# Three row blocks on four weight chunks at the start, an earlier weight load before the second attention, and two pinned orders

## The chip, the cores and the metric

The kernel runs on one core of a Trainium2 chip. The metric is the device time of one execution in microseconds (us); lower is better. The core has a matrix engine (TensorE; PE in the profile, its weight loads PEld), three other compute engines (VectorE = DVE, ScalarE = ACT, GpSimd = POOL) and SyncE (SP), whose queue issues most DMA transfers. Each engine runs its own instructions strictly in the order in which the program put them; semaphores tie the engines together.

## The reference

Two encoder layers on x of 1024 rows by 1024 columns, all in float32. Layer 0 mixes tokens by latent attention, layer 1 by differential attention; after each there is a gated feed-forward. What the change touches first is the first product of layer 0 and the normalisation behind it:

```python
h = x @ w_in                                   # 1024 x 704
c_q, c_kv, k_rope = jnp.split(h, [384, 640], axis=-1)
c_q = _rmsnorm(c_q, g_q)
c_kv = _rmsnorm(c_kv, g_kv)
...
h = _layernorm(ALPHA * h + mix, ln_mix_g[i], ln_mix_b[i])
h = _layernorm(ALPHA * h + _swiglu(h, ffn_w_gu[i], ffn_w_down[i]), ln_ffn_g[i], ln_ffn_b[i])
...
h = x @ w_in                                   # layer 1: 1024 x 3072, q, k and v of 8 heads
gate, up = jnp.split(x @ w_gu, 2, axis=-1)     # the feed-forward
return (jax.nn.silu(gate) * up) @ w_down
```

## The kernel before

**Precision.** TensorE multiplies in a rounded 32-bit format. Every operand is split into a rounded high part (a cast, nearly always on ACT) and the rest (a subtraction on DVE or POOL), and each product is made of three: high by high, high by low, low by high. So each operand costs a load, a cast and a subtraction before TensorE has all of it.

**First projection** (`load_x`, `load_w_in`, `project`, `latents`, `turn_c`). The 1024 rows are 8 row blocks of 128, and the 1024 columns of x are 8 chunks k of 128. One chunk of w_in is 128 x 704 (352 KB); one row block of x is 128 x 1024 (512 KB), laid out so that columns 128k to 128k+127 are the operand of chunk k. `project` accumulates a row block's 128 x 704 result in two PSUM banks, hq (384 columns, tag m) and hk (320 columns, tag t), with six matmuls for each chunk: xh by wh, xh by wl, xl by wh, for hq and hk each, so 48 for a row block. There are three banks of each of the tags m and t. Row blocks 0 and 1 are projected together, chunk by chunk; blocks 2 to 7 follow one at a time. The loads are issued by SP in program order: x of block 0 for chunks 0 and 1, w chunk 0 in two pieces, x of block 1 for chunks 0 and 1, w chunk 1, the rest of block 0, w chunk 2, the rest of block 1, w chunks 3 to 7. `latents` squares and sums hq and hk on ACT, scales them on DVE into a tile cn (two buffers) with a power on POOL between, and so frees the banks; `turn_c` transposes cn.

**Order.** The program is a list of operations; a scheduler that simulates the engines puts each engine's share in order at build time. `behind(i, j)` pins one operation behind another without a wait. `tc.high_priority` moves a part forward.

**End of layer 0.** `ffn` ends with eleven products of its last block (`dw` from the operands `op_w` and `op_h`), which POOL prepares from `t4` (L520) while `next_x` loads the first value weights of layer 1 (`wbv`). The rows of layer 0's result are normalised by `layer_norm` (L184 is its last step) and transposed by `to_xT` into the operand of layer 1 (`xTp_f`). The weights of head 0's query (tile `wb`) are loaded by `proj_b`, the first time it is called; the subtraction of that load (L137 on POOL) is pinned behind the power of the first normalised row block.

**Start of a feed-forward.** `load_pre` prepares the gate operands n = 0 to 5, `gates` multiplies them in pairs, `prepare` and `consume` do the rest of each n. One pin in `load_pre` puts the cast of operand 1 of n = 3 behind `ends["p1"]`, which is the last plain copy of a gate product.

Of the kernel before, what the change touches and what calls it, by code (L numbers as in the profile page):

```python
# [16 lines left out]
P = 128  # L17
S = 1024
D = 1024
# [23 lines left out]
def trunk(  # L43
# [54 lines left out]

    banks("ps0", PS_BUFS_A)
    dr = ctx.enter_context(tc.tile_pool(name="dr", bufs=1, space=DRAM))  # L100

# [26 lines left out]
    def load_w(src, cols, name, hi=None, lo=None, eng=None, raw=None, ins=False):  # L128

        if raw is None:  # L130
            raw = wp.tile([P, 1024], F32, tag="wr", bufs=2, name=f"r_{name}")
        nc.sync.dma_start(raw[:, :cols], src)
        if hi is None:
            hi = wp.tile([P, 1024], F32R, tag="wh", name=f"h_{name}")
            lo = wp.tile([P, 1024], F32R, tag="wl", name=f"l_{name}")
        A.copy(hi[:, :cols], raw[:, :cols])
        j = (eng or G).tensor_tensor(lo[:, :cols], raw[:, :cols], f32(hi[:, :cols]), ALU.subtract)  # L137
        return (hi, lo, j.ins) if ins else (hi, lo)
# [397 lines left out]
    def ffn(side, xo, xst, pending, layer, x_src, x_dst, lng, lnb, next_x, spare=()):  # L536
# [53 lines left out]
        def prepare(n, pr):  # L590
# [8 lines left out]
            if pr == ("5" if n < 2 else "6"):  # L599
                i = V.tensor_tensor(a21, a21, a22, ALU.add).ins  # L600
                if n < 2:
                    behind(i, ends["x"])
            if pr == ("3" if n < 2 else "6"):
                V.tensor_tensor(a11, a21, a11, ALU.subtract)
# [13 lines left out]
        def consume(n, pr):  # L618
# [3 lines left out]
            if pr in "12":  # L622
# [10 lines left out]
                else:  # L633
                    A.activation(g0, acc[n, "a"], AF.Silu)
                return
# [17 lines left out]
            if pr == "6":  # L653
                V.tensor_tensor(u2, p1, acc[n, "b"], ALU.add)
                for c in acc[n, "cs"] if n < 2 else ():
# [427 lines left out]
    with tc.tile_pool(name="a0", bufs=2, side="right") as pool:  # L1083
        xs, win = {}, []

        def load_x(tb, k0=0, k1=KD):

            if tb not in xs:
                xs[tb] = [
                    pool.tile([P, D], dt, tag=tag, name=f"{tag}_{tb}", bufs=2 if tag == "x" else 3)  # L1090
                    for dt, tag in ((F32, "x"), (F32R, "xh"), (F32R, "xl"))
                ]
            c = slice(k0 * P, k1 * P)
            xt, xh, xl = (t[:, c] for t in xs[tb])
            nc.sync.dma_start(xt, xt_in[tb, :, c])
            i, j = A.copy(xh, xt).ins, V.tensor_tensor(xl, xt, f32(xh), ALU.subtract).ins
# [4 lines left out]
        def load_w_in(k, n=1):  # L1101
# [4 lines left out]
            if n == 1:  # L1106
                *_, j = load_w(w_in_a[k], 704, f"win{k}", hi, lo, G if k > 2 and k % 2 else V, raw, True)
                return j
# [7 lines left out]
        load_w_in(0, 2)  # L1116
        load_x(1, 0, 2)
        load_w_in(1)
        load_x(0, 2, 8)
        load_w_in(2)  # L1120
        load_x(1, 2, 8)
        third = load_w_in(3)
        for k in range(4, KD):
            load_w_in(k)
        nc.sync.dma_start(ident, c_ident)
        with tc.issue_after(third):
# [5 lines left out]
        def project(tbs):  # L1132
            ms = [(ps_m(f"hq{tb}"), ps_t(f"hk{tb}")) for tb in tbs]
            for k in range(KD):
                kc = slice(k * P, (k + 1) * P)
                wh, wl = win[k]
                for tb, (hq, hk) in zip(tbs, ms):
                    _, xh, xl = xs[tb]
                    for lh, w, st, sp_ in (
                        (xh, wh, k == 0, False), (xh, wl, False, False), (xl, wh, False, k == KD - 1)  # L1140
                    ):
                        T.matmul(hq[:, :384], lh[:, kc], w[:, 0:384], start=st, stop=sp_)  # L1142
                        T.matmul(hk[:, :320], lh[:, kc], w[:, 384:704], start=st, stop=sp_)
            return ms

        def latents(tb, hq, hk):
            junk = pool.tile([P, 384], F32, tag="junk", name=f"junk{tb}")
            ssq = small(f"ssq{tb}", 2)
            A.activation(junk, hq[:, :384], AF.Square, accum_out=ssq[:, 0:1])
            ends["squares", tb] = A.activation(junk[:, :256], hk[:, :256], AF.Square, accum_out=ssq[:, 1:2]).ins  # L1150
            ve = small(f"cve{tb}", 2)
# [3 lines left out]
            G.tensor_tensor(rs, ve, mhalf, ALU.pow)  # L1155
            cn = pool.tile([P, 768], F32, tag="cn", name=f"cn{tb}")
            ra = pool.tile([P, 64], F32, tag="ra", name=f"ra{tb}")
# [22 lines left out]
        done = []  # L1180
        for tbs in ((0, 1), (2,), (3,), (4,), (5,), (6,), (7,)):
            for tb in tbs:
                if tb > 1:
                    load_x(tb)
# [8 lines left out]
    gs, nlam = cst[:, 16:17], cst[:, 24:25]  # L1193
    V.memset(ones, 1.0 / P)

    def constants():
# [14 lines left out]
    with ast as st:  # L1211
# [4 lines left out]
        for t, src in ((cos, c_cos), (sin, c_sin), (ba, c_bias_a)):  # L1216
            nc.sync.dma_start(t, src)
        vt, qr, qn, kn, wts, lt, pts = {}, {}, {}, {}, {}, {}, {}
# [127 lines left out]
    def next_x():  # L1346
        pool = xst.enter_context(tc.tile_pool(name="xp0", bufs=1, side="right", reuse_waits="tile"))
        wts["v", 0] = [load_w(w_b_v[0, kh], 1024, f"wbv0_{kh}") for kh in range(2)]
        return new_xT(pool, "f0")

# [17 lines left out]
    with ExitStack() as st:  # L1368
# [280 lines left out]
```

## Time and profile before

| what | value |
|---|---|
| median of 3 runs | 2256.71 us (2256.47 to 2257.42) |
| the profiled execution: its time | 2256.85 us |
| its span, first to last instruction | 2255.1 us |
| mean granted TensorE clock over the span | 0.999 |
| TensorE busy | 2235.1 us, 99% |
| DVE, ACT, POOL busy | 68%, 45%, 34% |
| share of the 16 DMA engines, mean rate | 35% and 128 GB/s |

The busy share says how much of the span an engine had an instruction under way; only TensorE is near the whole. So time can be won or lost only where TensorE waits or runs at a lower clock, and the rows in the section below show the few places where it does.

### The profile page before, as it was taken

The numbers are of one execution on the slowest core, as the hardware profiler recorded it, in microseconds if no ns is written. First come the engines' busy times: TensorE is split into PE (matmuls) and PEld (weight loads), VectorE is DVE, ScalarE is ACT, GpSimd is POOL, SyncE is SP. The second block draws the span as 40 slices with busy tenths as digits, with TensorE's granted clock in tenths as the row PEclk, the third lists the DMA queues.
The fourth block names the chain that finished last, engine by engine and source line by source line (L and its number), as shares of the span: only waits on it lengthen the run. The fifth ranks groups of instructions, "written<-read, shape, count | busy, mean of one in ns | idle before, by whom it ended". The sixth has DMA issues, their size and how long they took to land.

```text
span 2255.1 us, 31061 instructions
## 1 busy us (share of the span) xinstructions
PE 2235.1 (99%) x11410; PEld 1911.9 (85%) x11410; DVE 1543.9 (68%) x2894; ACT 1014.0 (45%) x2097; POOL 773.5 (34%) x626
## 2 busy tenths in 40 slices
PE   9999999999999999999999999999999999999998
PEld 8899998888888888888989898988888888888886
DVE  5676765696666657767576666577787656658778
ACT  4455664352333334444465656455432333334444
POOL 2232341114434440456432424222014444430551
PEclk9999999999999999999999999999999999999999
DMA  5010125334535338454310212063344232238453
GB/s 204 14 35 32 42 71 187 141 130 146 181 126 201 121 131 327 177 201 150 103 44 32 64 34 68 24 224 131 121 148 163 82 110 101 102 112 331 160 183 149
DMA packets 105545, 287.76 MB, mean 128 GB/s; under 512 B 7968, under 2 KB 30112, under 8 KB 94896
## 3 DMA queue, kind: packets, MB, share of 16 engines
q1 hardware_dynamic: 101552, 277.44, 34.6%
q0 software_dynamic: 3840, 8.33, 1.4%
q8 instruction: 90, 1.47, 0.3%
q14 instruction: 63, 0.52, 0.1%
HBM read 204.47 MB, written 77.07 MB: 125 GB/s over the span
## 4 chain that ended last, share of the span: by engine, by line
PE 96%; DVE 2%; DMA 1%; ACT 1%; issue 1%; POOL 0%; SPq 0%; DVEq 0%; POOLq 0%; ACTq 0%
PE gb L563 16%; PE gc L563 11%; PE ga L563 10%; PE dw L889 8%; PE dx L889 5%; PE zp_a L431 4%; PE s_a L220 3%; PE s_b L220 3%; PE dv L889 3%; PE dy L889 3%; PE bp L145 3%; PE bp L143 3%; PE bp L144 3%; PE o_a L263 2%; PE o_b L263 2%; PE hq L1142 2%
## 5 line engine op out<-in xcount | busy, mean ns | idle before, releaser
L519 ACT CAST op_g<-gr 128x512 fp32r<-128x512 f32 x240 | 146.8, 621 | 377.9 <-PE gb L563 185.8
L520 POOL TENSOR_TENSOR op_g<-gr,op_g 128x512 fp32r<-128x512 f32 x104 | 144.9, 1398 | 253.8 <-ACT op_g L519 141.6
L520 DVE TENSOR_TENSOR op_h<-rh,op_h 128x512 fp32r<-128x512 f32 x152 | 140.1, 948 | 51.1 <-ACT op_h L519 51.1
L563 PE MATMUL ga<-xh_m,op_g 128*128 128x512 f32 x512 | 168.2, 389 | 0.0
L889 PE MATMUL dw<-op_w_t,op_h 128*128 128x512 f32 x660 | 151.2, 390 | 0.0
L519 ACT CAST op_h<-rh 128x512 fp32r<-128x512 f32 x152 | 91.9, 619 | 124.3 <-PE dx L889 32.6
L889 PEld LDWEIGHTS dw<-op_w_t,op_h 128*128 128x128 f32 x660 | 123.6, 188 | 25.8 <-DVE op_h L520 0.3
L228 ACT ACTIVATE l_b<-l_b,mx_b 128x256 f32<-128x256 f32 (+7 forms) x128 | 99.4, 777 | 74.8 <-DVE mx_b L223 72.9
L520 DVE TENSOR_TENSOR op_g<-gr,op_g 128x512 fp32r<-128x512 f32 x136 | 112.9, 833 | 17.1 <-ACT op_g L519 16.8
L520 POOL TENSOR_TENSOR op_w_b<-rw_b,op_w_b 128x512 fp32r<-128x512 f32 x44 | 64.7, 1493 | 172.1 <-ACT op_w_b L519 172.0
L1451 POOL TENSOR_SCALAR l_b<-l_b,rb,cst 128x128 f32<-128x128 f32 (+3 forms) x64 | 52.5, 821 | 200.5 <-DVE rb L1450 188.0
L889 PE MATMUL dx<-op_w_b,op_h 128*128 128x512 f32 x528 | 120.3, 389 | 0.0
L889 PEld LDWEIGHTS dx<-op_w_b,op_h 128*128 128x128 f32 x528 | 99.1, 188 | 20.6
L563 PE MATMUL gb<-t2h_f,op_g 128*128 128x512 f32 x352 | 115.4, 390 | 0.4 <-DVE op_g L520 0.4
L563 PE MATMUL gc<-t1h_f,op_g 128*128 128x512 f32 x352 | 115.6, 389 | 0.0
L563 PE MATMUL gb<-t4h_f,op_g 128*128 128x512 f32 x352 | 115.5, 389 | 0.0
L563 PE MATMUL gc<-b22h_f,op_g 128*128 128x512 f32 x352 | 115.4, 389 | 0.0
L563 PE MATMUL gb<-t3h_f,op_g 128*128 128x512 f32 x352 | 115.2, 389 | 0.0
L563 PEld LDWEIGHTS ga<-xh_m,op_g 128*128 128x128 f32 x512 | 96.1, 188 | 19.9
L520 POOL TENSOR_TENSOR op_g<-s,op_g 128x512 fp32r<-128x512 f32 x40 | 55.2, 1381 | 166.5 <-ACT op_g L519 158.6
L143 PE MATMUL bp<-xT_f,h_wb 128*128 128x512 f32 x256 | 101.8, 398 | 0.0
L144 PE MATMUL bp<-xT_f,h_wb 128*128 128x512 f32 x256 | 101.6, 397 | 0.0
(389 smaller groups left out, 6689.5 us busy)
## 6 DMA issues: line engine op xcount, KB each, us to landing
gr<-in_w_gu SPq DMA_DIRECT2D x44, 1024.0 KB, 6.8
rh<-h_dr SPq DMA_DIRECT2D x28, 1024.0 KB, 4.8
h_dr<-sh SPq DMA_DIRECT2D x22, 1024.0 KB, 5.0
h_dr<-hp SPq DMA_DIRECT2D x22, 768.0 KB, 4.1
tt<-in_w_dn SPq DMA_DIRECT2D x22, 512.0 KB, 8.8
rh<-h_dr SPq DMA_DIRECT2D x12, 768.0 KB, 4.4
wo_dr<-op_pwo SPq DMA_DIRECT2D x16, 512.0 KB, 3.3
z<-xs_dr SPq DMA_DIRECT2D x16, 512.0 KB, 11.1
```

What stands on the lines that cost most here:

```text
L143: T.matmul(ps_out, lh, rh, start=(i == 0), stop=False)
L144: T.matmul(ps_out, lh, rl, start=False, stop=False)
L145: T.matmul(ps_out, ll, rh, start=False, stop=(i == n - 1))
L220: T.matmul(s[:, :w], lh, rh[:, ks], start=(j == 0), stop=(j == len(q_pass) - 1))
L228: ends["exp"] = A.activation(l[:, :n], l[:, :n], AF.Exp, bias=mx, scale=-1.0, accum_out=sm).ins
L263: T.matmul(po[:, c], a, b[:, j % 2, c], start=st, stop=sp_, skip_group_check=True)
L431: T.matmul(m, a[:, h, :], self.wo[h][w][:, c], start=(start and h == heads[0] and a is oh and w == 0), stop=(stop and h == heads[-1] and a ...
L519: turns["cast"] = A.copy(hi, src).ins
L520: return eng.tensor_tensor(lo, src, f32(hi), ALU.subtract).ins
L563: T.matmul(o, w[:, a, k * P:(k + 1) * P], x[b][:, k, :], start=(first and k == 0 and (a, b) == (0, 0)), stop=(k == 3 and a == 1), skip_gro ...
L889: T.matmul(o, h[:, a, c], w[:, b_], start=(first and (a, b_) == (0, 0)), stop=(last and a == 1), skip_group_check=True,).ins for a, b_ in ...
L1451: G.tensor_scalar(l1[:, :n], l1[:, :n], r[:, 1:2], nlam, ALU.mult, ALU.mult)
```

## The change

It has five parts. (1) Eight matmuls of the constant tile `ones` with itself (`spin`, 128 x 128, float32) stand at the head of TensorE's order; their result is used by nothing, and the memset of `ones` moves to the start. (2) Row blocks 0, 1 and 2 are projected together for chunks 0 to 3, and then one after the other for chunks 4 to 7; loads, casts and subtractions of x follow in smaller pieces, the low part of weight chunk 7 moves from POOL to DVE, and later loads (x of blocks 3 to 7, cos, sin, the bias) stand behind the last weight load. (3) The squares in `latents` go to the tile cn, not to a scratch tile; raw x has three buffers. (4) Head 0's query weights are loaded in `next_x`, with the value weights; the pin on their subtraction is gone. (5) In the feed-forward, the cast pinned behind `ends["p1"]` now stands behind the Silu of n = 0, and the addition that opens n = 3 stands behind the first reading of n = 1's product.

```diff
@@ trunk: start
     banks("ps0", PS_BUFS_A)
+    V.memset(ones, 1.0 / P)
+    spin = ps.tile([P, 512], F32, tag="s", bufs=ps_bufs[0], name="spin")
+    for _ in range(8):
+        T.matmul(spin[:, :P], ones, ones, start=True, stop=True)
@@ load_w
-        nc.sync.dma_start(raw[:, :cols], src)
+        ends["load"] = nc.sync.dma_start(raw[:, :cols], src).ins
+        if "w" in ends:
+            behind(ends["load"], ends["w"])
@@ ffn: prepare, pr == "6"
                 if n < 2:
                     behind(i, ends["x"])
+                elif n == 3:
+                    behind(i, ends["read"])
@@ ffn: consume, pr in "12" and pr == "6"
-                    A.activation(g0, acc[n, "a"], AF.Silu)
+                    i = A.activation(g0, acc[n, "a"], AF.Silu).ins
+                    if n == 0:
+                        ends["p1"] = i
...
-                V.tensor_tensor(u2, p1, acc[n, "b"], ALU.add)
+                i = V.tensor_tensor(u2, p1, acc[n, "b"], ALU.add).ins
+                if n == 1:
+                    ends["read"] = i
@@ the loads of the first projection
         load_x(0, 0, 2)
         load_w_in(0, 2)
         load_x(1, 0, 2)
+        load_x(2, 0, 2)
         load_w_in(1)
-        load_x(0, 2, 8)
+        for tb in range(3):
+            load_x(tb, 2, 4)
         load_w_in(2)
-        load_x(1, 2, 8)
         third = load_w_in(3)
+        for tb in range(3):
+            load_x(tb, 4, 8)
         for k in range(4, KD):
             load_w_in(k)
+        ends["w"] = ends["load"]
@@ project
-            for k in range(KD):
-                kc = slice(k * P, (k + 1) * P)
-                wh, wl = win[k]
-                for tb, (hq, hk) in zip(tbs, ms):
-                    _, xh, xl = xs[tb]
+            for k0 in (0, 4):
+                for k, i in itertools.product(range(k0, k0 + 4), range(len(tbs))) if k0 == 0 else (
+                    (k, i) for i in range(len(tbs)) for k in range(k0, k0 + 4)
+                ):
+                    kc = slice(k * P, (k + 1) * P)
+                    (wh, wl), (hq, hk), (_, xh, xl) = win[k], ms[i], xs[tbs[i]]
@@ the loop over row blocks
-        for tbs in ((0, 1), (2,), (3,), (4,), (5,), (6,), (7,)):
+        for tbs in ((0, 1, 2), (3,), (4,), (5,), (6,), (7,)):
@@ next_x
         wts["v", 0] = [load_w(w_b_v[0, kh], 1024, f"wbv0_{kh}") for kh in range(2)]
+        wts[0, 0] = load_w(w_b_qk[0, 0], 1024, "wb0_0")
@@ proj_b
-                *wts[which, h], i = load_w(w_b_qk[h, which], 1024, f"wb{h}_{which}", ins=True)
-                if len(wts) == 2:
-                    behind(i, normed[0][2])
+                wts[which, h] = load_w(w_b_qk[h, which], 1024, f"wb{h}_{which}")
```

Where the change moves instructions, the order of three engines shows it. The first place is TensorE at the very start; the digit behind a name is the row block (hq, hk, xh, xl) or the chunk (wih is the high part of the weights, wil the low part). Before:

```order
L1142 MATMUL hq0_194<-wih0_124,xh_0_119 128x384
L1143 MATMUL hk0_195<-wih0_124,xh_0_119 128x320
L1142 MATMUL hq0_194<-wil0_125,xh_0_119 128x384
L1142 MATMUL hq0_194<-wih0_124,xl_0_120 128x384
L1142 MATMUL hq1_196<-wih0_124,xh_1_134 128x384
...
L1143 MATMUL hk1_197<-wih0_124,xl_1_135 128x320
L1142 MATMUL hq0_194<-wih1_139,xh_0_119 128x384
```

And now, on the same engine at the same place:

```order
L103 MATMUL spin_78<-ones_62 128x128 x8
L1161 MATMUL hq0_222<-wih0_134,xh_0_129 128x384
L1164 MATMUL hk0_223<-wih0_134,xh_0_129 128x320
L1161 MATMUL hq0_222<-wil0_135,xh_0_129 128x384
L1161 MATMUL hq0_222<-wih0_134,xl_0_130 128x384
L1161 MATMUL hq1_224<-wih0_134,xh_1_144 128x384
...
L1161 MATMUL hq2_226<-wih0_134,xh_2_150 128x384
L1164 MATMUL hk2_227<-wih0_134,xh_2_150 128x320
...
L1164 MATMUL hk2_227<-wih0_134,xl_2_151 128x320
L1161 MATMUL hq0_222<-wih1_155,xh_0_129 128x384
```

The first four real matmuls and the fifth, which needs row block 1, are the same; chunk 1 now comes after eighteen matmuls on chunk 0, where it came after twelve.

The second place is DVE when the first row blocks are done: cve is the sum of squares made ready for the power, cn the scaled row block, and the row that writes cn from hq or hk is the last reader of that PSUM bank. Before:

```order
L1153 TENSOR_SCALAR cve0_298<-ssq0_295 128x1
...
L1164 SCALAR_TENSOR_TENSOR cn0_303<-hq0_194,crs0_301,gq_190 128x384
L1165 SCALAR_TENSOR_TENSOR cn0_303<-hk0_195,crs0_301,gk_192 128x256
L1096 TENSOR_TENSOR xl_3_433<-x_3_431,xh_3_432 128x1024
L1152 TENSOR_SCALAR cve1_317<-ssq1_314 128x1
```

Now:

```order
L1180 TENSOR_SCALAR cve0_376<-ssq0_373 128x1
...
L1179 TENSOR_SCALAR cve1_394<-ssq1_391 128x1
...
L1190 SCALAR_TENSOR_TENSOR cn0_372<-hq0_222,crs0_379,gq_218 128x384
L1190 SCALAR_TENSOR_TENSOR cn1_390<-hq1_224,crs1_397,gq_218 128x384
L1191 SCALAR_TENSOR_TENSOR cn0_372<-hk0_223,crs0_379,gk_220 128x256
L1191 SCALAR_TENSOR_TENSOR cn1_390<-hk1_225,crs1_397,gk_220 128x256
L1110 TENSOR_TENSOR xl_3_428<-x_3_426,xh_3_427 128x1024
```

The scaling of row block 0 now stands behind the sums of row block 1, and the low part of x for row block 3 behind both scalings.

The third place is POOL at the end of layer 0: l_wbv are the low parts of the first value weights, l_wb those of head 0's query weights, op_w0_t4 those of the last products' operands, rs_f0 the power of the normalisation. Before:

```order
L137 TENSOR_TENSOR l_wbv0_1_10047<-r_wbv0_1_10044,h_wbv0_1_10046 128x1024
L520 TENSOR_TENSOR op_w0_t4_2_9858<-rw0_t4_0_9817,op_w0_t4_2_9858 128x512
...
L520 TENSOR_TENSOR op_w0_t4_10_10018<-rw0_t4_2_9977,op_w0_t4_10_10018 128x512
L181 TENSOR_TENSOR rs_f0_0_10130<-ve_f0_0_10128,cst_63 128x1
L137 TENSOR_TENSOR l_wb0_0_10335<-r_wb0_0_10332,h_wb0_0_10334 128x1024
```

Now:

```order
L143 TENSOR_TENSOR l_wbv0_1_10060<-r_wbv0_1_10057,h_wbv0_1_10059 128x1024
L143 TENSOR_TENSOR l_wb0_0_10066<-r_wb0_0_10063,h_wb0_0_10065 128x1024
L526 TENSOR_TENSOR op_w0_t4_2_9871<-rw0_t4_0_9830,op_w0_t4_2_9871 128x512
...
L526 TENSOR_TENSOR op_w0_t4_10_10031<-rw0_t4_2_9990,op_w0_t4_10_10031 128x512
L187 TENSOR_TENSOR rs_f0_0_10149<-ve_f0_0_10147,cst_63 128x1
```

The subtraction of the query weights has moved ahead of nine operands of the last products; on ACT their cast has moved to the same place, ahead of the cast of `op_w0_t4_2`, and on SP their load ahead of the last pieces of h and of the down weights.

## Rows read from the trace of the kernel before

**Rows 1.** Waits of TensorE: us in total, times, longest; first and fifth of nine.

```profile
PE hq L1142 <- ACT wih L1111: 4.4, 1, 4.4
...
PE xTp_f L148 <- DVE y_f L184: 0.7, 1, 0.7
```

**Rows 2.** Windows, two stretches: us, busy (x) by engine, clock, DMA share, GB/s.

```profile
12.00:18.00 6.00, 6.00 (x39) 6.00 (x38) 3.68 (x3) 2.62 (x4) 5.05 (x5) 1.00 1.03 419
...
1615.00:1690.00 75.00, 75.00 (x340) 62.30 (x339) 63.93 (x101) 37.03 (x67) 11.82 (x9) 1.00 0.46 161
```

**Rows 3.** Timeline of the first 20 us: start us, us, engine, line, operation.

```profile
0.89 0.17 DVE L1194 MEMSET ones<- 128x128 f32 x1
...
5.83 0.53 PE L1142 MATMUL hq<-wih,xl 128*128 128x384 f32 x1
...
6.99 0.40 ACT L1096 CAST xh<-x 128x256 fp32r<-128x256 f32 x1 [1.97 <-DMA x<-in_xt]
...
7.85 0.78 ACT L136 CAST wih<-wraw 128x704 fp32r<-128x704 f32 x1 [0.46 <-DMA wraw<-in_w_in_a]
```

**Rows 4.** The chain that ended last, first 12 us: start us, us, what.

```profile
2.12 4.85 DMA x<-in_xt
...
7.44 0.69 PE hq L1142
...
11.01 0.27 PE hk L1143
...
11.57 0.15 PE hk L1143
11.72 0.18 PE hq L1142
```

**Rows 5.** Timeline of TensorE, 1187 us: the only plain float32 products.

```profile
1187.69 1.07 PE L1482 MATMUL ms<-sq,ones 128*128 128x512 f32 x2
...
1188.83 0.39 PE L145 MATMUL bp<-xT_f,l_wb 128*128 128x512 f32 x1
1189.06 0.40 PE L143 MATMUL bp<-xT_f,h_wb 128*128 128x512 f32 x1
```

**Rows 6.** The chain again, at 1041 us: fourteen 128 x 128 float32 transposes.

```profile
1041.52 1.53 PE xTp_f L148 x14
```

**Rows 7.** Timeline of ACT, 28 us: the first squares of row block 0.

```profile
28.24 0.49 ACT L1149 ACTIVATE junk<-hq 128x384 f32<-128x384 f32 x1 [3.37 <-PE hq L1142]
```

**Rows 8.** Timeline of DVE, 29 to 32 us: `latents` of row block 0.

```profile
29.36 0.15 DVE L1153 TENSOR_SCALAR cve<-ssq 128x1 f32<-128x1 f32 x1 [0.35 <-ACT junk L1150]
...
30.35 0.62 DVE L1164 SCALAR_TENSOR_TENSOR cn<-hq,crs,gq 128x384 f32<-128x384 f32 x1
...
31.28 1.22 DVE L1096 TENSOR_TENSOR xl<-x,xh 128x1024 fp32r<-128x1024 f32 x1
```

**Rows 9.** Timeline of DVE, 1078 to 1085 us: two last steps of `layer_norm`.

```profile
1078.68 2.74 DVE L184 SCALAR_TENSOR_TENSOR y_f<-y_f,rs_f,gb_f 128x1024 f32<-128x1024 f32 x1
...
1083.73 1.29 DVE L184 SCALAR_TENSOR_TENSOR y_f<-y_f,rs_f,gb_f 128x1024 f32<-128x1024 f32 x1
```

**Rows 10.** Timeline of POOL, 1041 to 1081 us: low parts of weights and operands.

```profile
1041.42 2.85 POOL L137 TENSOR_TENSOR l_wbv<-r_wbv,h_wbv 128x1024 fp32r<-128x1024 f32 x1
1045.63 1.55 POOL L520 TENSOR_TENSOR op_w_t<-rw_t,op_w_t 128x512 fp32r<-128x512 f32 x1 [1.36 <-ACT op_w_t L519]
...
1077.92 2.42 POOL L137 TENSOR_TENSOR l_wb<-r_wb,h_wb 128x1024 fp32r<-128x1024 f32 x1
```

**Rows 11.** Timeline of TensorE, 1049 us: two transposes between high and low products.

```profile
1049.29 0.38 PE L148 MATMUL xTp_f<-ident,z 128*128 128x128 f32 x2
```

**Rows 12.** DMA issues, 1036 to 1060 us: count, KB each, median us to landing.

```profile
xs_dr<-z SPq DMA_DIRECT2D x1, 512.0 KB, 3.0
r_wb<-in_w_b_qk SPq DMA_DIRECT2D x1, 512.0 KB, 7.3
```

**Rows 13.** Timeline of ACT, 1624 us: the Silu of n = 0.

```profile
1624.04 0.60 ACT L634 ACTIVATE pg<-ga 128x512 f32<-128x512 f32 x1 [0.32 <-PE ga L563]
```

More of the change, by code (lines that the diff above doesn't have):

```diff
@@ L1089, in load_x @@
                 xs[tb] = [
-                    pool.tile([P, D], dt, tag=tag, name=f"{tag}_{tb}", bufs=2 if tag == "x" else 3)
+                    pool.tile([P, D], dt, tag=tag, name=f"{tag}_{tb}", bufs=3)
                     for dt, tag in ((F32, "x"), (F32R, "xh"), (F32R, "xl"))
@@ L1094, in load_x @@
             xt, xh, xl = (t[:, c] for t in xs[tb])
-            nc.sync.dma_start(xt, xt_in[tb, :, c])
+            i = nc.sync.dma_start(xt, xt_in[tb, :, c]).ins
+            if tb > 2:
+                behind(i, ends["w"])
             i, j = A.copy(xh, xt).ins, V.tensor_tensor(xl, xt, f32(xh), ALU.subtract).ins
@@ L1106, in load_w_in @@
             if n == 1:
-                *_, j = load_w(w_in_a[k], 704, f"win{k}", hi, lo, G if k > 2 and k % 2 else V, raw, True)
+                *_, j = load_w(w_in_a[k], 704, f"win{k}", hi, lo, G if k in (3, 5) else V, raw, True)
                 return j
@@ L1141, in project @@
                     ):
-                        T.matmul(hq[:, :384], lh[:, kc], w[:, 0:384], start=st, stop=sp_)
-                        T.matmul(hk[:, :320], lh[:, kc], w[:, 384:704], start=st, stop=sp_)
+                        j = T.matmul(hq[:, :384], lh[:, kc], w[:, 0:384], start=st, stop=sp_).ins
+                        if k > 3 and i and (k, lh, w) == (4, xh, wh):
+                            behind(j, last)
+                        h = T.matmul(hk[:, :320], lh[:, kc], w[:, 384:704], start=st, stop=sp_).ins
+                        if k > 3 and i and (k, lh, w) == (4, xh, wh):
+                            behind(h, last)
+                        if k == KD - 1 and lh is xl:
+                            last = h
             return ms
         def latents(tb, hq, hk):
-            junk = pool.tile([P, 384], F32, tag="junk", name=f"junk{tb}")
+            cn = pool.tile([P, 768], F32, tag="cn", name=f"cn{tb}")
             ssq = small(f"ssq{tb}", 2)
-            A.activation(junk, hq[:, :384], AF.Square, accum_out=ssq[:, 0:1])
-            ends["squares", tb] = A.activation(junk[:, :256], hk[:, :256], AF.Square, accum_out=ssq[:, 1:2]).ins
+            A.activation(cn[:, :384], hq[:, :384], AF.Square, accum_out=ssq[:, 0:1])
+            ends["squares", tb] = A.activation(
+                cn[:, 384:640], hk[:, :256], AF.Square, accum_out=ssq[:, 1:2],
+            ).ins
             ve = small(f"cve{tb}", 2)
@@ L1155, in latents @@
             G.tensor_tensor(rs, ve, mhalf, ALU.pow)
-            cn = pool.tile([P, 768], F32, tag="cn", name=f"cn{tb}")
             ra = pool.tile([P, 64], F32, tag="ra", name=f"ra{tb}")
@@ L1180, in trunk @@
         done = []
-        for tbs in ((0, 1), (2,), (3,), (4,), (5,), (6,), (7,)):
+        for tbs in ((0, 1, 2), (3,), (4,), (5,), (6,), (7,)):
             for tb in tbs:
-                if tb > 1:
+                if tb > 2:
                     load_x(tb)
@@ L1193, in trunk @@
     gs, nlam = cst[:, 16:17], cst[:, 24:25]
-    V.memset(ones, 1.0 / P)
     def constants():
@@ L1216, in trunk @@
         for t, src in ((cos, c_cos), (sin, c_sin), (ba, c_bias_a)):
-            nc.sync.dma_start(t, src)
+            behind(nc.sync.dma_start(t, src).ins, ends["w"])
         vt, qr, qn, kn, wts, lt, pts = {}, {}, {}, {}, {}, {}, {}
```

## The prediction

> **What bounds the kernel now.** I read the page first and then the waits of TensorE. In the waits the reader should look for time that a change can still take away, and there is little: 4.4 us until the first weight chunk is cast, and 0.7 us in the second layer where the transposes of its first row block wait for the last step of the normalisation [rows 1]. The windows confirm it from the other side: TensorE fills all of 12 to 18 us, while the first loads still run the DMA engines at 1.03 of their share, and all of 1615 to 1690 us, which holds the start of the last feed-forward [rows 2]. So wherever TensorE is full, making an operand earlier is worth nothing; a gain has to come from its few waits or from its clock. A shift won at the start does arrive at the end, because what follows is one chain of TensorE work.
>
> The third view, timeline and chain of the first 12 us, shows the clock. From 7.44 us on TensorE has work without a pause, but hk takes 0.27 us until about 11.4 us and 0.15 us from 11.57 us on, and hq 0.18 us there [rows 4]. The granted clock of the window from 12 us is 1.00 [rows 2], which is the 2.4 GHz level; twice the length before it is the 1.2 GHz level. Ahead of the rise lies a pause: the fourth matmul starts at 5.83 us and lasts 0.53 us, so it ends at 6.36 us [rows 3], and the fifth starts at 7.44 us [rows 4], since x of row block 1, issued at 2.12 us, lands 4.85 us later at 6.97 us [rows 4] and is cast from 6.99 us on for 0.40 us [rows 3].
>
> **Part 1, the spin.** The trace has plain float32 products in one place, ms with `ones`. Two records with 512 columns each make one of them; from 1187.69 us to 1188.83 us run that pair and one ordinary product, which takes 1189.06 - 1188.83 = 0.23 us, so the pair takes 1.14 - 0.23 = 0.91 us [rows 5], at the higher level. A quarter of the columns: 0.23 us, at the lower level 0.46 us, eight of them 3.65 us. The lower bound is that a spin costs what a float32 transpose of the same size does, 1.53 / 14 = 0.11 us [rows 6], at the lower level 0.22, eight 1.75 us. I take 3.65 us, since the spin is a product and not a transpose. The memset of `ones` ends at 0.89 + 0.17 = 1.06 us [rows 3]; now it is DVE's first, so the spin runs from about 1.1 to 4.75 us (bound 2.9 us). The first real matmul could start at 4.39 us (the wait of 4.4 us, [rows 1]); it loses up to 0.36 us, and the four that can run end at 6.36 + 0.36 = 6.72 us. They hide this before 7.44 us, with 0.7 us to spare; uncovered it would cost 0.36 us.
>
> So TensorE would now be busy from 1.1 to 6.7 us, 5.6 us without a pause, where before 2.0 us of work stood ahead of the pause. Before, the rise came behind unbroken work since 7.44 us. I therefore take the clock to be at the higher level by 7.44 us. Thirteen matmuls, six hq and seven hk, lay between 7.44 and 11.57 us, 4.13 us. At the higher level they take 6 x 0.175 + 7 x 0.15 = 2.10 us, and the first of them is longer by its start, 0.69 us [rows 4] where 0.32 would be usual at the lower level, half of it 0.17 at the higher: 2.27 us. **Term: -1.86 us**, bounds 0 (the rise comes when it did) and -1.86.
>
> The Trainium skill bears on this ("TensorE: Matmul & The Clock Gate", Part 1: The HAM clock gate): the half rate is the default, sustained activity of the array releases it and idleness brings it back. By that page, too, the spin helps if its activity runs into the real work, which ends in 2254.2 us; if the pause that is left counts as idleness, it does nothing, which ends in rival B's 2256.0 us. The trace agrees in the one thing that it shows, the rise behind unbroken work.
>
> **Part 2, three row blocks.** The loads of the first four matmuls are unchanged, and so is the fifth matmul's: x of block 1 stands fourth on SP as before. I keep 7.44 us. It could land sooner, since 128 KB of x follow it now where 352 KB of weights did; the pause of 1.08 us bounds that gain, and I take nothing, as most of its 4.85 us is before those compete. Does the faster TensorE outrun the loads? Chunk 1 is wanted after 18 matmuls, 14 of them behind 7.44 us: 7.44 + 14 x 0.1625 + 0.17 = 9.9 us. Its cast started at 7.85 us and took 0.78 us [rows 3]; with 128 KB ahead of it, at 419 GB/s [rows 2] 0.31 us, it ends at about 8.95 us. From there a chunk of 18 matmuls takes 2.9 us, and its 352 KB and three pieces of x of 64 KB, 544 KB, take 1.3 us. The loads keep ahead; if not, the lack can take back no more than the 1.86 us.
>
> At the end of the three blocks row block 3 needs xl, and DVE makes it behind the scaling of block 1. From the squares (28.24 us [rows 7]) to the sums 1.12 us, to the first scaling 0.99 us more, xl after 0.93 us more, for 1.22 us [rows 8]. Blocks 0 and 1 are done earlier than block 2 by one and two shares of 24 matmuls (3.9 us), so the scaling of both, four steps, ends about when block 2 does, and xl is ready some 1.3 to 1.5 us behind that. TensorE's order has eight matmuls on xh (1.3 us) and six transposes (0.7 us) ahead of the first that reads xl, 2.0 us. Spare 0.5 us; **term 0**, bound +1.2 us, the length of xl. That squares go to cn and x has three buffers changes where data lies, no time.
>
> **Part 4, the query weights.** TensorE's 0.7 us wait [rows 1] comes from the step L184: 2.74 us at 1078.68 us, where a later one takes 1.29 us [rows 9]. What runs beside the long one is POOL's low part of the query weights, from 1077.92 us for 2.42 us [rows 10]; it is moved away. L184 would be 1.45 us shorter, and the whole wait goes. **Term: -0.7 us**, bounds 0 (the cast or the sums ahead of that step are late next) and -0.7.
>
> What the new place costs: the work stands behind the second value weights, POOL 1041.42 + 2.85 = 1044.27 us [rows 10]. The load would be issued at about 1039.8 us, one transfer on SP's queue where little else waits; like xs_dr, of the same size in this stretch, it should land 3.0 us later, at 1042.8 us; the bound is the 7.3 us that it took in its old place [rows 12]. Then POOL does it in 2.42 to 2.85 us, until 1046.7 to 1047.1 us, and the low part of operand 2, which stood at 1045.63 us, follows for 1.55 us, until 1048.2 to 1048.7 us. TensorE wants it behind two transposes, 1049.29 + 2 x 0.11 = 1049.5 us [rows 6, 11]. Spare 0.8 to 1.3 us, **term 0**. With a landing after 7.3 us: 1047.1 us, cast 1.1 (0.40 us for 256 columns, 0.78 for 704 [rows 3]), POOL 2.42 to 2.85, operand 2 1.55: 1052.2 to 1052.6 us, 2.7 to 3.1 us too late.
>
> A page speaks against this place: the Trainium skill ("SBUF — State Buffer", section SBUF: two separate sides) says that a DVE step with two inputs in SBUF and a GpSimd step that reads SBUF take a shared port in turns, the later one standing still. The long L184 beside L137 agrees [rows 9, 10]; by the page the subtraction could do the same to DVE's work at 1045 us, which is the same price as the late landing at most.
>
> **Parts 3 and 5.** The order of the later loads only lets the weights pass. The cast that was tied to the plain copy now waits for the Silu, which ends at 1624.64 us [rows 13]; TensorE is full throughout [rows 2], with 24 matmuls of 0.23 us (5.5 us) to go before it reaches that operand, and a cast like the Silu's 0.60 us and a low part of 1.55 us [rows 10] fit under them. Zero; without this cover at most +2.2 us.
>
> **The sum.** The profiled execution took 2256.85 us, 0.14 above the median 2256.71. 2256.85 - 1.86 - 0.7 = 2254.3; against the median 2254.2.
>
> **The rivals.**
> A, the forecast: the clock is up at 7.44 us. 2254.2 us.
> B, the clock rises when it did. For it: the pause of 0.7 to 1.1 us before 7.44 us stays, and before the change 2.0 us of work ahead of it did not lift the clock. Against it: work ahead of the pause is nearly three times as long now. It would also follow if the spin is only 1.75 us long, which leaves a second pause from 2.9 to 4.39 us. 2256.71 - 0.7 = 2256.0 us.
> C, on the other side: the query weights land late in their new place, so that operand 2 comes 2.7 to 3.1 us late. 2254.2 + 3.1 = 2257.3 us, slower than before by 0.6. A stall begins with a landing after 1044.0 us, and it decides from one at about 1046.6 us, 6.8 us after the issue, where it has eaten both gains; the DMA queues are nearly idle there, which speaks against it, the old 7.3 us for it.
> D, xl of row block 3 is late: 2254.2 + 1.2 = 2255.4 us at most.
>
> **How the numbers follow.** A 0.62, B 0.22, C 0.07, D 0.09. A's own range is 2253.1 us (x of block 1 lands sooner by the whole pause) to 2254.9 (the clock rises a little late, the 0.7 us come half). With B at 2256.0 and D inside, and some 0.5 us by which runs of one kernel differ (those of before spread over 0.95), the range is 2253.0 to 2256.6; C is left out, with a part of the ends. About 0.2% (4.5 us) is what a measurement of this kernel can tell from no change. No case reaches 2252.2 us or 2261.2 us; I leave 0.07 for faster, from work that I did not see at the ends of stages, and 0.03 for slower.
>
> **What would show it.** Right: the first timeline shows eight spins of 0.46 us or less from about 1.1 us, the fifth real matmul near 7.44 us, and hk 0.15 us right behind it; no wait on xl of row block 3; L184 near 1.3 us with the wait of 0.7 us gone; L137 of the query weights ends before 1047.7 us in the old count of time. Wrong: hk of 0.27 us until 11 us (B); a wait of dw on op_w near 1050 us (C); a wait of hq on xl near 28 us (D). A gain over 3 us would mean that the pause at 6.4 us closed too; none at all, that a new wait ate both terms.

## The result and the profile after

The changed kernel takes 2259.86 us (median of 22 runs, 2257.14 to 2262.40), the kernel before 2256.68 us (22 runs on the same chips, 2255.03 to 2257.42). The ratio is 1.0015, with a 95% interval of 1.0009 to 1.0021: slower by 3.2 us, less than the 0.2% named above and still clear of no change. Forecast were 2254.2 us, in a range of 2253.0 to 2256.6 us.

Where the time went can be read from four landmarks on TensorE, transposes that both kernels have: of y_a and z_a (rows of the attention's result, ahead of each feed-forward), and of z and y_f (rows of layer 0's result). The view by tile gives the first and the last start of each. Before:

```profile
L148 PE MATMUL xTp_f<-ident,z x32: 270/272/273, 1041.4 to 1073.9; 128*128 128x128 f32 x32
L148 PE MATMUL xTp_f<-ident,y_f x32: 272/273/329, 1081.5 to 1099.0; 128*128 128x128 f32 x32
L148 PE MATMUL xTp_a<-ident,z_a x64: 270/272/273, 1552.9 to 1624.6; 128*128 128x128 f32 x64
...
L148 PE MATMUL xTp_a<-ident,y_a x8: 270/272/273, 451.8 to 452.6; 128*128 128x128 f32 x8
```

After:

```profile
L154 PE MATMUL xTp_f<-ident,z x32: 270/272/273, 1041.0 to 1078.3; 128*128 128x128 f32 x32
L154 PE MATMUL xTp_f<-ident,y_f x32: 272/273/275, 1084.6 to 1102.1; 128*128 128x128 f32 x32
L154 PE MATMUL xTp_a<-ident,z_a x64: 270/272/273, 1556.1 to 1627.8; 128*128 128x128 f32 x64
...
L154 PE MATMUL xTp_a<-ident,y_a x8: 270/272/273, 449.8 to 450.6; 128*128 128x128 f32 x8
```

The differences between one landmark and the next, with the end of the span (2255.1 and 2259.3 us), cut the program into five stretches. The table has them for the two kernels and, as what was lost or won against before, for the experiments told below; each is one profiled execution.

| us | start to first y_a | feed-forward 0, to first z | handoff, to first y_f | layer 1, to last z_a | feed-forward 1, to the end |
|---|---|---|---|---|---|
| before | 451.8 | 589.6 | 40.1 | 543.1 | 630.5 |
| after | 449.8 | 591.2 | 43.6 | 543.2 | 631.5 |
| after less before | -2.0 | +1.6 | +3.5 | +0.1 | +1.0 |
| part 4 undone | -3.0 | +1.6 | 0.0 | +0.1 | +1.0 |
| part 5 undone | -2.9 | +0.3 | +3.5 | +0.1 | -0.3 |
| both undone | -2.0 | +0.2 | 0.0 | +0.3 | +0.2 |
| query weights split by DVE | -3.8 | +1.8 | -0.5 | +0.1 | +1.0 |
| first pin alone (second undone) | -2.7 | +0.3 | +2.3 | 0.0 | +1.5 |
| second pin alone (first undone) | -1.4 | +1.8 | +2.3 | +0.3 | +0.5 |
| query weights split in POOL's idle time, no pins | -3.2 | +0.4 | -0.9 | 0.0 | +0.7 |

So in this execution the start won 2.0 us, near the forecast, and three stretches gave 6.1 us away. The first column needs care: the kernels in it have the same start and read -1.4 to -3.8 us, for a reason told in the section on why the prediction was wrong. The waits of TensorE point at the losses (us in total, times, longest):

```profile
PE dw L901 <- DVE op_h L526: 2.4, 1, 2.4
...
PE spin L103 <- DVE cst L109: 1.0, 1, 1.0
PE gb L569 <- DVE op_g L526: 0.8, 3, 0.4
PE hq L1161 <- DVE xl L1110: 0.6, 1, 0.6
```

The old waits on wih, xh and y_f [rows 1] are gone. New are one long wait of the last products of layer 0 (dw) on an h operand's low part, short ones of gb at the start of the feed-forwards, and one on xl of row block 3. Without the last, which belongs to the start, the new waits make some 3.2 of the 6.1 us; the rest is a lower clock and starts of matmuls that come later by too little for this list.

**The start.** In the chain of the first 12 us (start us, us, what) the spin runs from 1.05 us on for 3.79 us, the fifth real matmul starts at 6.39 us, and hk is 0.14 us long right behind it, where before it was 0.27 us up to 11 us [rows 4]:

```profile
1.05 3.79 PE spin L103 x16
4.83 0.32 PE hq L1161
...
6.39 0.58 PE hq L1161
6.97 0.14 PE hk L1164
```

**The handoff.** The timeline at 1043 us shows POOL at work without a break from 1044.72 to 1054.16 us, first on the query weights and then on four operands. Beside it DVE's six additions take 9.58 us; before, the same six took 5.17 us (first line below). The low parts of h behind them start at 1052.95 us, and TensorE stands for 2.39 us:

```profile
1043.76 5.17 DVE L865 TENSOR_TENSOR rw_t<-rw_t,tt 128x512 f32<-128x512 f32 x6
...
1043.45 9.58 DVE L877 TENSOR_TENSOR rw_t<-rw_t,tt 128x512 f32<-128x512 f32 x6
1043.59 1.05 ACT L142 CAST h_wb<-r_wb 128x1024 fp32r<-128x1024 f32 x1 [4.41 <-DMA r_wb<-in_w_b_qk]
...
1044.72 2.65 POOL L143 TENSOR_TENSOR l_wb<-r_wb,h_wb 128x1024 fp32r<-128x1024 f32 x1 [0.76 <-ACT h_wb L142]
1047.33 6.83 POOL L526 TENSOR_TENSOR op_w_t<-rw_t,op_w_t 128x512 fp32r<-128x512 f32 x4
...
1052.95 2.95 DVE L526 TENSOR_TENSOR op_h<-rh,op_h 128x512 fp32r<-128x512 f32 x3
```

And there is a second loss behind that stand, the clock's. In the windows (us, busy by engine, granted clock, DMA share, GB/s) the clock of the 3.3 us after it is 0.50, the 1.2 GHz level:

```profile
1052.00:1054.60 2.60, 0.37 (x2) 0.00 (x0) 2.60 (x2) 0.47 (x1) 2.10 (x2) 1.00 0.00 0
1054.60:1057.90 3.30, 3.15 (x7) 2.51 (x8) 1.30 (x3) 0.00 (x0) 0.00 (x0) 0.50 0.62 197
```

**The gain of part 4** came as forecast: the step that took 2.74 us [rows 9] takes 1.27 us, and the wait of 0.7 us is gone:

```profile
1082.58 1.27 DVE L190 SCALAR_TENSOR_TENSOR y_f<-y_f,rs_f,gb_f 128x1024 f32<-128x1024 f32 x1
```

**The feed-forward.** In the timeline of layer 0's feed-forward DVE stands for 1.32 us ahead of the first reading of n = 1's product (L664), since the second pin of part 5 keeps the addition of n = 3 (among the L606 rows) behind it. From there on DVE is behind, and at 495 us TensorE waits for it. Late as it is, DVE then meets POOL's work: its subtractions at 496.10 and 501.39 us take 1.77 us each, where with the pins undone (below) the same two take 0.68 us each:

```profile
488.99 0.69 DVE L664 TENSOR_TENSOR tmp<-pg,gb 128x512 f32<-128x512 f32 x1 [1.32 <-PE gb L569]
489.59 2.38 DVE L606 TENSOR_TENSOR gr<-gr 128x512 f32<-128x512 f32 x2
...
495.02 0.50 PE L569 MATMUL gb<-t4h_f,op_g 128*128 128x512 f32 x1 [0.18 <-DVE tmp L670]
496.10 1.77 DVE L526 TENSOR_TENSOR op_g<-gr,op_g 128x512 fp32r<-128x512 f32 x1
```

### The profile page after: what moved, and what is told of

It reads as the page before. It is cut to its first block, busy times and chain, and to the rows that moved or that the text cites. A ratio compares the mean times of both kernels' runs of the same rounds, so it can differ in the third digit from the quotient of the medians.

```text
span 2259.3 us, 31109 instructions
## 1 busy us (share of the span) xinstructions
PE 2240.6 (99%) x11426; PEld 1914.3 (85%) x11426; DVE 1555.9 (69%) x2899; ACT 1015.2 (45%) x2101; POOL 778.0 (34%) x625
## 4 chain that ended last, share of the span: by engine, by line
PE 92%; DVE 4%; DMA 1%; issue 1%; ACT 1%; POOL 1%; SPq 0%; DVEq 0%; POOLq 0%; ACTq 0%
PE gb L569 14%; PE ga L569 10%; PE gc L569 10%; PE dw L901 7%; PE dx L901 5%; PE zp_a L437 4%; PE s_a L226 4%; PE s_b L226 3%; PE dv L901 3%; PE dy L901 3%; PE bp L151 3%; PE bp L149 3%; PE bp L150 3%; PE o_a L269 2%; PE o_b L269 2%; PE hq L1161 1%
## 5 line engine op out<-in xcount | busy, mean ns | idle before, releaser
L526 DVE TENSOR_TENSOR op_g<-gr,op_g 128x512 fp32r<-128x512 f32 x136 | 118.0, 871 | 19.0 <-ACT op_g L525 18.8
```

What stands on the lines that cost most here:

```text
L526: return eng.tensor_tensor(lo, src, f32(hi), ALU.subtract).ins
```

## The experiments

The theory after the result has two halves. T4: in its new place the subtraction of the query weights on POOL holds up DVE, TensorE stands, and the clock falls. T5: the pins of part 5 make DVE late in both feed-forwards. The rival to both: the earlier start has moved transfers against work, and the losses follow from that.

**Part 4 undone.** The load goes back into `proj_b`, with its pin.

```diff
-        wts[0, 0] = load_w(w_b_qk[0, 0], 1024, "wb0_0")
...
+                *wts[which, h], i = load_w(w_b_qk[h, which], 1024, f"wb{h}_{which}", ins=True)
+                if len(wts) == 2:
+                    behind(i, normed[0][2])
```

> The changed kernel with part 4 undone: head 0's query weights load and split where they did before. Theory T4 (in the new place the subtraction on POOL keeps DVE's six additions at 1043 us long, 9.58 us instead of 5.17, the low part of an h operand comes late, TensorE stands 2.4 us and then runs at the 1.2 GHz level for 3.4 us): the 4.3 us lost there come back and the 0.9 us won at the handoff go, so 3.4 us less than the changed kernel, about 2256.5 us, with no granted clock under 1.00 between 1040 and 1060 us. Rival: that stall comes from the shift of the start and not from the moved weights: then it stays, 2260 us or a little more.

Measured: 2257.29 us (11 runs), ratio to before 1.0004 (0.9995 to 1.0012), 2.6 us less than the changed kernel, where 3.4 us were expected. The intervals of the two ratios overlap a little (1.0009 to 1.0012); the trace is the clearer witness: the six additions take 5.17 us again, the long wait is gone, the handoff costs 40.1 us as before. T4 holds for the place; the rival, that the stall would stay, falls.

**Part 5 undone.** Both pins as before.

```diff
-                elif n == 3:
-                    behind(i, ends["read"])
...
-                    if n == 0:
-                        ends["p1"] = i
```

> The changed kernel with part 5 undone: both pins in the feed-forward as before. Theory T5 (DVE stands behind the first reading of n = 1's product, its additions for n = 3 come late, and TensorE loses some 1.4 us at the start of each of the two feed-forwards): 2.9 us less than the changed kernel, about 2257.0 us, with the short waits of gb on DVE at 495 to 507 us and 1671 to 1687 us gone. Rival: those waits come from transfers that the earlier start has moved: they stay, 2259.9 us.

Measured: 2256.63 us (11 runs), ratio 1.0000 (0.9991 to 1.0009), 3.2 us less than the changed kernel. Both feed-forwards lose nothing worth naming (+0.3 and -0.3 us in the table), so T5 holds for the two pins together and the rival falls here too. In the time in which DVE stood, it now makes two operands' sums of n = 3 ahead of the reading (which is L660 here):

```profile
487.40 0.69 DVE L616 TENSOR_TENSOR s<-gr 128x512 f32<-128x512 f32 x1
488.01 0.68 DVE L612 TENSOR_TENSOR gr<-gr 128x512 f32<-128x512 f32 x1
488.62 0.68 DVE L660 TENSOR_TENSOR tmp<-pg,gb 128x512 f32<-128x512 f32 x1
...
492.99 0.68 DVE L526 TENSOR_TENSOR op_g<-gr,op_g 128x512 fp32r<-128x512 f32 x1
```

The stand at 1052 us and the clock's fall behind it are there in this kernel too.

**Both undone,** which leaves the start, parts 1 to 3.

> The changed kernel with parts 4 and 5 undone, so parts 1 to 3, the start, alone. If T4 and T5 are both right their costs add: 2259.9 - 3.4 - 2.9 = 2253.6 us, which is 3.1 us less than before, and the trace keeps the start's gain of 2.4 us less 0.9 us for the late xl of row block 3 up to the end. Rival: the start's gain is given back later whatever else is changed: 2256.7 us, as before.

Measured: 2254.59 us (11 runs), ratio 0.9991 (0.9983 to 1.0000). The costs add, as far as runs can tell: 2.6 + 3.2 = 5.8 us, and 2259.86 - 2254.59 = 5.3 us. The start alone is 2.0 us faster than before; the interval touches no change.

**The query weights split by DVE,** in the new place.

```diff
-        wts[0, 0] = load_w(w_b_qk[0, 0], 1024, "wb0_0")
+        wts[0, 0] = load_w(w_b_qk[0, 0], 1024, "wb0_0", eng=V)
```

> The changed kernel with one edit: the subtraction of head 0's query weights, in its new place, on DVE and not on POOL. If the loss there is POOL and DVE holding each other up (T4), the six additions on DVE take about 5.2 us again, the subtraction 1.2 to 2.4 us behind them, the h operand is ready at about its need, TensorE stands 0 to 0.5 us and keeps its clock: about 2256 us. If it is the work itself that comes too early, wherever it is done, DVE is late by the same 2.4 us and the clock falls again: about 2260 us.

Measured: 2256.04 us (11 runs), ratio 1.0000 (0.9991 to 1.0008), 3.8 us less than the changed kernel. DVE has 1.21 us more to do and is done sooner; TensorE's list of waits has none on an operand of dw. DVE's timeline:

```profile
1041.73 5.16 DVE L877 TENSOR_TENSOR rw_t<-rw_t,tt 128x512 f32<-128x512 f32 x6
1046.82 1.21 DVE L143 TENSOR_TENSOR l_wb<-r_wb,h_wb 128x1024 fp32r<-128x1024 f32 x1
1047.96 5.19 DVE L526 TENSOR_TENSOR op_h<-rh,op_h 128x512 fp32r<-128x512 f32 x3
```

So it is not the early work that harms but where it is done: POOL and DVE at once. The Trainium skill ("SBUF — State Buffer", section SBUF: two separate sides) calls the port that they share an exclusive lock; the trace agrees, with 9.58 us against 5.16 us for the same six additions.

**The start without the spin,** parts 1 to 3 less eight products.

```diff
-    spin = ps.tile([P, 512], F32, tag="s", bufs=ps_bufs[0], name="spin")
-    for _ in range(8):
-        T.matmul(spin[:, :P], ones, ones, start=True, stop=True)
```

> The start alone (parts 1 to 3, measured at 2254.6 us) without the eight products of the spin. If the clock is what the start wins, hk is 0.27 us long again until about 10 to 11 us and some 1.9 us go: about 2256.5 us. If three row blocks on shared chunks are what wins, it stays at about 2254.6 us.

Measured: 2256.05 us (11 runs), ratio 0.9998 (0.9989 to 1.0007); the start alone stood at 0.9991. In the chain hk stays at 0.27 us up to 10.9 us, and falls to 0.14 us behind it:

```profile
10.63 0.27 PE hk L1157
10.89 0.23 PE hq L1154
11.12 0.14 PE hk L1157
```

**The spin alone,** in the kernel before (the three lines above added to it, and the memset moved).

> The kernel before with the spin as its one edit, row blocks and loads as before. If the clock alone is worth it and the loads of two row blocks keep ahead: hk 0.15 us from 7.4 us on, 1.9 us less, about 2254.7 us. If two row blocks use up each chunk too fast for the loads at the 2.4 GHz level, TensorE waits for weights between 8 and 14 us and gives back most of it: about 2256.3 us.

Measured: 2255.89 us (11 runs), ratio 1.0002 (0.9994 to 1.0011). The clock is up by 6 us, but x of row block 1 comes no sooner, and TensorE, done earlier, waits longer for it, 1.7 us instead of 1.1 [rows 3, 4]:

```profile
PE hq L1146 <- ACT xh L1100: 1.7, 1, 1.7
```

Three delays of 0.2 to 0.3 us at products on a weight's low part follow up to 14 us. In its trace it leads before by 1.0 us at the end, which the runs do not show. So neither half of the start differs from the kernel before by more than its interval. The two together stand at 0.9991, with 1.0000 as the upper end; whether each half wins a little or only both together do, these runs cannot tell apart.

**Filling the stand,** first attempt: seven unused products ahead of the waiting matmul, and its control with the order alone.

```diff
+                if fill and j == 3:
+                    f = ps_s("fill")
+                    for _ in range(7):
+                        i = T.matmul(f[:, :P], ones, ones, start=True, stop=True).ins
+                        behind(i, done[3][1])
+                    for tb in range(4):
+                        behind(done[tb][2], i)
```

> The changed kernel with seven unused products of `ones` (0.23 us each, 1.6 us) on TensorE where it stands and waits for the h operand at 1053 us, and three of the four matmuls behind the wait that need no late operand drawn ahead of it. If the clock falls because TensorE stands, it now stays at 1.00 from 1040 to 1060 us and the 1.7 us (3.4 us at half) come back: about 2258.2 us, in spite of more work. If the fall has another cause, it is there again: 2259.9 us or a little more.

> The same as the filled kernel without the seven products: the order of the four matmuls alone. TensorE then waits some 1.7 us in one piece. If that is still enough for the clock to fall, about 2259.9 us; if it is too short for it, about 2258.2 us, and the filled kernel shows nothing.

Measured: 2263.97 us (5 runs, 1.0035, 1.0022 to 1.0047) and 2258.49 us (11 runs, 1.0010, 1.0001 to 1.0019). The filled kernel is no test of the filling: the unused products take a PSUM bank of the tag (s) that the transposes of z use, these start at 1060.7 us where they started at 1041.0 us, and TensorE waits for POOL first:

```profile
1047.93 3.93 PE L901 MATMUL dw<-op_w_t,op_h 128*128 128x512 f32 x16 [0.88 <-POOL op_w_t L526]
```

It adds one case of the clock all the same: TensorE stands later, for 2.46 us up to 1064.76 us, and behind that the clock is at 0.50:

```profile
1062.30:1064.70 2.40, 0.00 (x1) 0.00 (x0) 2.40 (x4) 0.23 (x1) 1.55 (x1) 1.00 0.00 0
1066.20:1069.50 3.30, 3.30 (x9) 2.53 (x9) 0.69 (x1) 1.14 (x2) 1.27 (x1) 0.50 0.00 0
```

In the control TensorE stands for 1.69 us and the clock does not fall in the profiled run:

```profile
1056.00:1060.00 4.00, 3.91 (x17) 3.22 (x18) 1.24 (x3) 1.14 (x2) 1.29 (x1) 1.00 0.63 211
```

**Filling it without a bank:** ten products of a zero tile, added to the sums that the next matmul writes, so that TensorE's order stays.

```diff
+                for _ in range(fill if a else 0):
+                    T.matmul(o[:, :P], zero, ones, start=False, stop=False, skip_group_check=True)
```

> The changed kernel with ten products of a zero tile (0.23 us each, 2.3 us, added to the same sums, which they leave as they are) on TensorE directly ahead of the matmul that waits 2.4 us for the h operand; TensorE's order is otherwise the same. If the clock falls because TensorE stands there, it stays at 1.00 from 1052 to 1060 us and 1.2 to 1.7 us come back although TensorE has more to do: about 2258.4 us. If the fall has nothing to do with the standing, 2259.9 us or a little more, with the clock at 0.50 for a part of that stretch.

Measured: 2261.77 us (10 runs), ratio 1.0023 (1.0014 to 1.0032), 1.9 us more than the changed kernel. Half of the expectation came: behind the filled stand the clock stays at 1.00. As the fall does not come in every execution (see one pin at a time), this one profile does not prove that the filling kept it away. The time did not come back, because the order on DVE is another: at 1061 us three additions stand ahead of the next low parts of h, where the changed kernel makes one addition and then the operand. TensorE waits 2.17 us for that operand, and the clock falls behind this stand (0.72 as a mean of the last window):

```profile
1052.00:1056.00 4.00, 3.86 (x28) 3.40 (x27) 3.80 (x4) 0.36 (x1) 1.98 (x2) 1.00 0.11 12
...
1062.00:1066.00 4.00, 1.83 (x8) 1.20 (x8) 4.00 (x6) 1.14 (x2) 1.45 (x1) 1.00 0.03 12
1066.00:1072.00 6.00, 6.00 (x21) 4.74 (x20) 1.12 (x2) 1.60 (x3) 1.28 (x1) 0.72 0.01 3
```

DVE there, first in this kernel and then in the changed one:

```profile
1061.49 2.06 DVE L878 TENSOR_TENSOR rw_t<-rw_t,tt 128x512 f32<-128x512 f32 x3 [5.69 <-DMA rw_t<-in_w_dn]
1063.48 2.95 DVE L527 TENSOR_TENSOR op_h<-rh,op_h 128x512 fp32r<-128x512 f32 x3
...
1061.68 0.69 DVE L877 TENSOR_TENSOR rw_t<-rw_t,tt 128x512 f32<-128x512 f32 x1 [5.77 <-DMA rw_t<-in_w_dn]
1062.29 1.78 DVE L526 TENSOR_TENSOR op_h<-rh,op_h 128x512 fp32r<-128x512 f32 x1
```

**One pin at a time.** First the second pin undone, then the first.

> The changed kernel with only the second pin of part 5 undone (the addition that opens n = 3 no longer stands behind the first reading of n = 1's product); the cast still stands behind the Silu. If that addition's place on DVE is the whole price of part 5, all 3.2 us that both pins cost (changed kernel 2259.9, without both 2256.6 us) come back: about 2256.7 us, no waits of gb on DVE's tmp at 495 us. If the cast behind the Silu costs something of its own, less comes back, down to 2259.9 us.

> The changed kernel with only the first pin of part 5 undone (the cast stands behind the plain copy again); the addition that opens n = 3 still stands behind the first reading of n = 1's product. If that addition's place on DVE costs what both pins together cost in the first feed-forward (1.4 us, DVE standing 1.3 us ahead of the reading), the waits of gb at 495 and 507 us stay and the second feed-forward loses about as much: about 2259.9 us. If the two pins only cost together, the waits go: about 2256.7 us.

Measured: 2259.40 us (1.0013, 1.0005 to 1.0022) and 2259.55 us (1.0015, 1.0006 to 1.0024), 11 runs each: no single pin, taken away, gives the 3.2 us back. The table shows why. The second pin costs all of feed-forward 0 (+1.8 with it alone, +0.3 without it). In feed-forward 1 the first pin alone costs 1.5 us, in one wait that neither kernel had. The second pin's 0.5 us there is not clear, as kernels without either pin read -0.3 to +0.7 us in that column:

```profile
1669.89 0.47 PE L569 MATMUL gb<-t3h_f,op_g 128*128 128x512 f32 x1 [1.62 <-ACT tmp L692]
```

These two runs also price the clock: TensorE stands for 2.4 us in both, the clock does not fall in either profile, and the handoff loses 2.3 us instead of 3.5 us. The profile of the kernel with the first pin alone is its fastest run (2258.22 us, median 2259.40), so other runs of it may have had the fall; no trace shows that.

**The query weights in POOL's idle time,** with the pins undone: loaded early, subtracted behind the last operand.

```diff
-        wts[0, 0] = load_w(w_b_qk[0, 0], 1024, "wb0_0")
+        *wts[0, 0], i = load_w(w_b_qk[0, 0], 1024, "wb0_0", ins=True)
+        behind(i, turns["last"])
```

> The start alone (2254.6 us) with head 0's query weights loaded early as in part 4, but their subtraction on POOL pinned behind the low part of the last operand, into POOL's idle time at 1067 to 1077 us. If T4 is right in that only POOL's work beside DVE's additions was harmful, no stall at 1050 us, no wait of 0.7 us at the handoff, L184 at 1.3 us: 0.7 to 0.9 us less, about 2253.8 us. If the early load itself harms (the buffers, the queue), 2256 us or more.

Measured: 2253.84 us (11 runs), ratio 0.9990 (0.9981 to 0.9998). The subtraction runs where POOL had nothing to do, and the handoff wins 0.9 us:

```profile
1064.83 2.41 POOL L143 TENSOR_TENSOR l_wb<-r_wb,h_wb 128x1024 fp32r<-128x1024 f32 x1
```

**Two more on top:** the low part of x of row block 3 let go from the pin behind the scaling (`if tb > 3:` ahead of it), and, by itself, DVE's subtraction without the pins of part 5.

> The kernel with the subtraction in POOL's idle time, and one edit more: the low part of x for row block 3 no longer stands behind the scaling of row block 0 on DVE, so that it is made 1 to 2 us sooner. If TensorE's wait of 0.6 us for it at 32 us is lost time: about 2253.1 us, and no wait of hq on xl. If the scalings that it passes are late in its place (they free the banks of row blocks 3 and 4): about 2253.8 us, with a wait on them.

> The changed kernel with the subtraction of head 0's query weights on DVE and without the two pins of part 5. If both costs are separate they add: 2256.0 - 3.2 = 2252.8 us. If DVE's extra 1.2 us at 1047 us is only hidden by the time lost in the feed-forward, 2254 us or more, with a wait of dw near 1051 us.

Measured: 2253.48 us (0.9989, 0.9980 to 0.9998) and 2253.51 us (0.9989, 0.9980 to 0.9997), 11 runs each. Both are 2.5 us faster than the kernel before by the ratio, the best of this study. The edit on xl shows nothing: the wait of hq on xl is absent, but it is absent without the edit too, in the kernel above, and xl starts at 29.20 us here and at 29.28 us there, not 1 to 2 us sooner. Its 0.4 us against the kernel above may be chance.

## Why the prediction was wrong

**The spin and the clock: right.** Its length was taken as 3.65 us and measured 3.79 us; the clock was up before the fifth matmul. **The start as a whole: right in size, in part by luck.** -1.86 us were forecast for the clock alone, with the fifth matmul at 7.44 us. It came at 6.39 us, within the bound given but at nothing in the sum, and row block 3 took 0.9 us back, also at nothing in the sum, so that 2.0 us arrived. That last is rival D, with another cause than argued: not the order on DVE but POOL beside it. In the changed kernel two low parts of x on DVE take 5.40 us while POOL splits weights for 4.63 us; two of 1.22 us [rows 8] would be 2.4 us. The second pair of lines is from the run with part 4 undone, where DVE came first:

```profile
28.91 4.63 POOL L143 TENSOR_TENSOR l_wa<-r_wa,h_wa 128x896 fp32r<-128x896 f32 x2 [1.39 <-ACT h_wa L142]
...
29.22 5.40 DVE L1110 TENSOR_TENSOR xl<-x,xh 128x1024 fp32r<-128x1024 f32 x2
...
29.05 2.35 DVE L1110 TENSOR_TENSOR xl<-x,xh 128x1024 fp32r<-128x1024 f32 x2
...
29.39 5.55 POOL L143 TENSOR_TENSOR l_wa<-r_wa,h_wa 128x896 fp32r<-128x896 f32 x2 [2.03 <-ACT h_wa L142]
```

It is a race that falls differently from profile to profile; with one profile of each kernel, what decides it stays open. Of the thirteen profiles with three row blocks and this order, six have POOL's split start first: DVE's two low parts then take 4.9 to 5.6 us, and the first landmark comes 0.7 to 2.2 us ahead of before. In the seven in which DVE starts first they take 2.35 us, TensorE has no wait on xl, and the landmark comes 2.7 to 3.8 us ahead. Two of the six are also held back by a late clock, one for want of the spin, one in spite of it.

**Part 4, the gain: right,** 0.7 us forecast, 0.9 us measured where nothing else disturbs it. **Part 4, the new place: wrong,** and it is the step "Spare 0.8 to 1.3 us, term 0". The load landed in time and operand 2 was ready in time, as worked out there. What the step left out is the other engine: it followed POOL's own work alone, and worked out nothing of what DVE does beside it. DVE had six additions to make at 1043 us and the low parts of h behind them. The price that the text put on POOL and DVE holding each other up stood beside the sum and not in it, as no more than rival C's 3.1 us, and C's chance counted the landing alone. The row that showed the effect was on the page all the time: 2.74 us against 1.29 us [rows 9], the reason for the gain, is the same collision. The change moved it from a place where it cost 0.7 us to one where it costs 4.4 us (3.5 us net of the 0.9).

**The clock's fall** was in no case of the prediction. It adds about 1.2 us (3.5 less 2.3) when it comes, which is also what takes the loss of 4.4 us past the 3.1 us that were called the most.

**Part 5: wrong** in the step "Zero". The cover of the first pin was worked out for one operand of one feed-forward; the second pin, the addition behind a reading, got no price at all. "TensorE is full throughout" [rows 2] says that the operands came in time so far, not by how much: DVE, 1.3 us late, had no slack to give. Together the pins cost 3.2 us of the median (2259.86 less 2256.63).

The five stretches add up to the 4.2 us between the two profiled executions because they divide the span; that is no test. The test is in the runs: without part 4 the kernel is 2.6 us faster, without part 5 3.2 us, without both 5.3 us. Left open: why the first pin alone costs a wait only in the second feed-forward, and how much of the loss in the first is DVE's stand and how much the work of POOL that it meets behind it.

## What to carry to other kernels

When work moves on one of DVE and GpSimd, list what the other does in the same microseconds, and put the collision into the sum: the stall that a move cures shows what it will cost at its new place. A pin that holds a step behind a wait also holds all that stands behind that step on its engine, so its price is the slack of that engine, which a full TensorE does not show. Idle time of an engine, found in its timeline, is the place for work that can go anywhere.

## What was not expected of the hardware

TensorE's clock fell to 1.2 GHz behind stands of 2.2 to 2.5 us, but not behind each: it fell in the profiles of the changed kernel and of the one with part 5 undone (2.4 us each) and of the two filled kernels (2.46 and 2.17 us), and not in those with one pin (2.4 us each). The Trainium skill ("TensorE: Matmul & The Clock Gate", Part 1: The HAM clock gate) says that idleness brings the half rate back; the traces agree in that all four falls come behind such a stand, and show that the same stand can pass without one. The rise at the start differs as well: with the same spin hk was 0.14 to 0.15 us from about 7 us on in all profiles but one, the control above, where it was 0.27 us up to 10.2 us:

```profile
10.20 0.27 PE hk L1168
10.47 0.25 PE hq L1165
10.72 0.15 PE hk L1168
```
